# Raising the rank of all splits out of PSUM and of the heads' sums, in a two-layer transformer block on one core

## The chip, the cores and the metric

The kernel runs on one core of a Trainium2 chip. The metric is the time of one execution in device microseconds. Five engines work side by side, each through a queue of its own in order: TensorE (PE, the matrix engine, with its weight loads PEld), VectorE (DVE), ScalarE (ACT), GpSimd (POOL) and SyncE (SP), which here only issues DMA transfers. Matrix products are accumulated in PSUM; everything else lies in SBUF.

## The reference

Two layers of a hybrid block over a latent stream x of 512 tokens (8 rows of a grid of 64 columns) and a context stream of 256 tokens, 1024 features each. Cut to what matters:

```python
h  = modulate(rms_norm(x, norm_pre1), sh1, sc1)        # adaln sums from c @ w_ada
q, k, v, u, cq, ckv, kr, g = split_cols(h @ w_in, IN_SIZES)
o_na   = na_latent(q, k, v, k_ctx, v_ctx, rpb)         # 8 heads of 64: window 8x16, and the context
o_pool = pool_mixer(u, pool_w, pool_scale)
o_mla  = mla_attend(q_nope, q_rope, k_nope_all, k_rope_all, v_all)   # 8 heads, 768 keys
y = merge_branches(o_na, o_pool, o_mla, g) @ w_o       # sigmoid gates
x = x + g1 * rms_norm(y, norm_post1)
h2 = modulate(rms_norm(x, norm_pre2), sh2, sc2)
x = x + g2 * rms_norm(conv_ffn(h2), norm_post2)        # up to 2*2816, conv of 3, gelu, down
```

The context stream goes through the same in the first layer; in the second only its keys and values are used.

## The kernel before

Products need nearly float32 accuracy, so each operand is split in two float32r tiles: hi, a rounding of the value, and lo, what is left. A product is three matmuls (hi by lo, hi by hi, lo by hi). A split is a pair: ScalarE casts hi, then VectorE subtracts hi from the value to give lo. `evac` does this for a value that lies in PSUM (in the last merge, for one in SBUF). `split` does it for weights and other values in SBUF, with the subtraction on VectorE or GpSimd by an estimate of their queues.

The order is made in two steps. While the program is written out, the class `Sched` keeps a rough clock and interleaves generators: streams of attention units, a dense stream (`dense`, a projection is 24 matrix steps over 512 and 256 tokens), and a background stream that sums up the next adaln vectors on VectorE (`adacc`, `adahi`, `adalo`). The order in which TensorE's instructions are written is the order that it keeps (`manual_schedule` for PE). For all other engines and the DMA queue a planner, when the kernel is built, plays the program through with its own estimates: at each moment it gives an engine the instruction of lowest rank among those that it believes ready. The rank is the place in the text. `tc.high_priority(HP)` with HP = 100 ranks what it encloses 100 places earlier. The queues that result are fixed; on the chip each engine waits for the first instruction in its own.

Stages of a layer, in order, with the names of the profile:

- pooling branch (ups, pwps) with gates (gps) and its merge (mps);
- windowed attention, 8 heads: q, k, v (qps, kps, vps), v transposed (vtps, split to vt). A unit has scores S, softmax in P (maxima mx, sums sx, their reciprocal rs; Pc for context units), four transposes of P (tps), a split to PT, and products ops (opc) which hold both halves of a head's output in 64 partitions each. `gather` adds them: ScalarE copies one half to osum, VectorE adds the other. Three streams of units run at a time. S, tps, ops, opc and vtps share four PSUM buffers ("p1"); projections have two of their own ("mm");
- gates and merge of that branch (tgn, acn); latent projections (cps);
- second attention (MLA), 8 heads over 768 keys: projections in pieces pps, split to qh and ql, kh and kl; V. A score unit has S in the two "mm" buffers, a maximum mxm on VectorE, an exponential P<-S on ScalarE, and a scaling P<-P on ScalarE, VectorE or GpSimd. `apply` transposes P (tps), splits it to pth and ptl, and makes po, whose halves are added in om (copy o on ScalarE, sum on VectorE). tps, pps, rps and po share four buffers;
- merge (mps, acm, split to mhi and mlo), output projection yps with its square sq and scaled y, and a chain for each 128 tokens: xt, square, rstd on GpSimd, ht, eight transposes hps, split to mhi and mlo. The first FFN products f2ps begin as soon as 256 tokens are there;
- FFN (ffps, cv, gh and gl, dps), and the same token chain at its end.

In the kernel before, raised ranks stand in the scores (`na_unit`, `na_ctx_unit`, `scores`) and at sq and y of the output projection. The splits of `evac` and the sums in `gather` and `apply` have the plain rank.

Of the kernel before, what the change touches and what calls it, by code (L numbers as in the profile page):

```python
# [8 lines left out]
F32 = mybir.dt.float32  # L9
F32R = mybir.dt.float32r  # L10
AF = mybir.ActivationFunctionType
ALU = mybir.AluOpType
# [13 lines left out]
HP = 100  # L26
# [215 lines left out]
def body(tc, I, out):  # L242
    sch = Sched()
    nc = _NC(sch, tc.nc)
    es = ExitStack()

    def mm(out, lhsT, rhs, start, stop):
        n = 1
        for d in rhs.shape[1:]:
            n *= d  # L250
        sch.pe(max(n, 256) * 0.4167 + 2.5 if rhs.dtype == F32R else max(n, 16) * 1.667, out.name, [lhsT.name, rhs.name])
        nc.tensor.matmul(out=out, lhsT=lhsT, rhs=rhs, start=start, stop=stop)  # L252

    def tr(out, in_):
        sch.pe(109, out.name, [in_.name])
        nc.tensor.transpose(out=out, in_=in_, identity=ident)  # L256
# [126 lines left out]
                yield 0  # L383

    def evac(ps, hi, lo, scale=None):
        if scale is None:
            nc.scalar.copy(out=hi, in_=ps)
            nc.vector.tensor_sub(out=lo, in0=ps, in1=hi.bitcast(F32))
        else:
            nc.scalar.activation(out=hi, in_=ps, func=AF.Copy if isinstance(scale, float) else AF.Identity, scale=scale)  # L390
            nc.vector.scalar_tensor_tensor(out=lo, in0=ps, scalar=scale, in1=hi.bitcast(F32),
                                           op0=ALU.mult, op1=ALU.subtract)

    def rstd_of(ss, ss2=None):
        r = sm.tile([128, 1], F32, tag="rstd", name="rstd")
# [70 lines left out]
    def norm_to_h(xt, A, B, pool, hhi, hlo, tt):  # L466
        ss = sm.tile([128, 1], F32, tag="ss", name="ss")
        t = pool.tile([128, D], F32, tag="ht", bufs=2, name="ht")
        nc.scalar.activation(out=t, in_=xt, func=AF.Square, accum_out=ss)
        r = rstd_of(ss)  # L470
        nc.vector.scalar_tensor_tensor(out=t, in0=xt, scalar=r, in1=A, op0=ALU.mult, op1=ALU.mult)
        nc.vector.tensor_add(out=t[:, :BC], in0=t[:, :BC], in1=B[:, :BC])
        nc.gpsimd.tensor_add(out=t[:, BC:], in0=t[:, BC:], in1=B[:, BC:])
        for g in range(2):
            yield Need([t], [P1])
            ps = ps1.tile([128, 512], F32, tag="p1", name="hps")
            for k in range(4):
                tr(ps[:, k * 128:(k + 1) * 128], t[:, (4 * g + k) * 128:(4 * g + k + 1) * 128])
            pv = ps.rearrange("p (k c) -> p k c", k=4)
            evac(pv, hhi[:, 4 * g:4 * g + 4, tt * 128:(tt + 1) * 128], hlo[:, 4 * g:4 * g + 4, tt * 128:(tt + 1) * 128])  # L480
# [6 lines left out]
    def transpose_n(P, n):  # L487
        ps = ps1.tile([128, 512], F32, tag="p1", name="tps")
        for i in range(n):
            tr(ps[:, i * 128:(i + 1) * 128], P[:, i * 128:(i + 1) * 128])  # L490
        return ps
# [158 lines left out]
    for l in range(NL):  # L650
# [79 lines left out]
        def pool_mix(g):  # L730
            def run(_):
                ps = pmm.tile([128, 1024], F32, tag="mm", name="pwps")
                yield from mm3(ps, *pool_d[g], 1, TQ)
                evac(ps[:, :TQ], ophi[:, g], oplo[:, g], pscale[:, g:g + 1])
            return run
# [43 lines left out]
        def na_vt(p):  # L779
            def run(_):  # L780
                v = qkvt[p, "v"]
                vt = na.tile([128, 10, 2, 2, 64], F32R, tag="vt", bufs=2, name="vt")
                srcs = [v[:, 8 * BAND0[j] + 128 * hf:8 * BAND0[j] + 128 * hf + 128] for j in range(4) for hf in range(2)]
                srcs += [v[:, SX + i * 128:SX + (i + 1) * 128] for i in range(2)]
                for i0 in range(0, 10, 4):
                    tp = ps1.tile([128, 512], F32, tag="p1", name="vtps")
                    n = min(4, 10 - i0)
                    for i in range(n):
                        tr(tp[:, i * 128:(i + 1) * 128], srcs[i0 + i])
                    tv = tp[:, :n * 128].rearrange("p (k e c) -> p k e c", k=n, e=2)  # L790
                    evac(tv, vt[:, i0:i0 + n, :, 0, :], vt[:, i0:i0 + n, :, 1, :])
                qkvt[p, "vt"] = vt
                yield 0
            return run
# [17 lines left out]
        def gather(po, e, hi, lo, shape):  # L812

            t = na.tile([128, 512], F32, tag="osum", bufs=1, name="osum")
            rows = slice(64 * e, 64 * e + 64)
            nc.scalar.copy(out=t[0:64], in_=po[64:128])
            nc.vector.tensor_add(out=t[0:64], in0=po[0:64], in1=t[0:64])
            v = t[0:64].rearrange("p (u h c) -> p u h c", u=2, h=2)
            o = na.tile([128, 2, 128], F32, tag="ohead", bufs=1, name="ohead")
            nc.gpsimd.tensor_add(out=o[rows], in0=v[:, :, 0, :], in1=v[:, :, 1, :])  # L820
            ov = shape(o[rows])
            nc.scalar.copy(out=hi[rows], in_=ov)
            nc.vector.tensor_sub(out=lo[rows], in0=ov, in1=hi[rows].bitcast(F32))

        def na_unit(p, e, j):
# [35 lines left out]
            if left[u] == 0:  # L861
                c = slice(4 * (j // 2), 4 * (j // 2) + 4)
                gather(ops, e, rowm(nahi[:, p, :SX])[:, c], rowm(nalo[:, p, :SX])[:, c],
                       lambda x: x.rearrange("p u (b r c) -> p (u b) r c", b=2, r=8))
# [225 lines left out]
        om = mp.tile([128, 4, TQ], F32, tag="om", name="om")  # L1090
# [146 lines left out]
        def apply(hd, qp):  # L1237
            e = hd % 2
            wide = qp < 2
            us = [(hd, qp, 0), (hd, qp, 1)] if wide else [(hd, qp, None)]  # L1240
            yield lambda: all(u in ptile for u in us)
            Ps = [ptile[u] for u in us]
            pth, ptl = [ml.tile([128, 6, 256], F32R, tag=t, bufs=2, name=t) for t in ("pth", "ptl")]
            nkt = 6 if wide else 2
            if wide:
                for q2 in range(2):
                    yield Need([Ps[q2]], [P1])
                    tp = transpose_n(Ps[q2], 4)
                    tv = tp.rearrange("p (k c) -> p k c", k=4)
                    evac(tv, pth[:, 0:4, q2 * 128:(q2 + 1) * 128], ptl[:, 0:4, q2 * 128:(q2 + 1) * 128])  # L1250
            yield Need(Ps, [P1])
            tp = ps1.tile([128, 512], F32, tag="p1", name="tps")
            for i in range(2):
                for q2 in range(2):
                    c0 = (4 + i) * 128 if wide else q2 * 256 + i * 128
                    tr(tp[:, (2 * i + q2) * 128:(2 * i + q2 + 1) * 128], Ps[q2 if wide else 0][:, c0:c0 + 128])
            evac(tp.rearrange("p (k c) -> p k c", k=2), pth[:, nkt - 2:nkt], ptl[:, nkt - 2:nkt])
            flow["t"] += len(us)
            yield Need([pth, ptl], [P1])
            rn = slice(64 * e, 64 * e + 64)  # L1260
            po = ps1.tile([128, 512], F32, tag="p1", name="po")
            n = 0
            k0 = 0 if wide else 4
            for i in range(nkt):
                for t in (pth, ptl):
                    mm(out=po[:, 0:256], lhsT=V[:, k0 + i, hd, :], rhs=t[:, i, :], start=n == 0, stop=n == 2 * nkt - 1)
                    n += 1
            o1 = ml.tile([128, 256], F32, tag="o1", bufs=1, name="o1")
            nc.scalar.copy(out=o1[0:64], in_=po[64:128, 0:256])
            nc.vector.tensor_add(out=om[rn, hd // 2, qp * 256:qp * 256 + 256], in0=po[0:64, 0:256], in1=o1[0:64])  # L1270
            yield 0

        def sstream():
# [7 lines left out]
        def tstream():  # L1281
            yield lambda: "v" in hready
            while pairs_:
                yield from apply(*pairs_.pop(0))
# [403 lines left out]
```

## Time and profile before

| | us |
|---|---|
| median of 3 runs | 2472.48 (2471.0 to 2478.62) |
| the profiled execution's own time | 2472.59 |
| its span, first to last instruction | 2470.8 |
| PE busy | 2380.2 |
| DVE busy | 1530.0 |
| ACT busy | 1029.2 |
| POOL busy | 643.3 |

The mean granted TensorE clock is 0.99. Busy times of engines overlap. A group of rows names tiles as out<-in; L252 is the line of the helper that issues matmuls, L256 that of transposes, L207 that of all instructions which go through the recording wrapper, so tiles tell them apart.

### The profile page before, as it was taken

How to read it: one execution, taken by the hardware profiler on the slowest of the kernel's cores; microseconds unless marked ns; L12 is line 12 of the kernel's file. 1: busy time of each engine (PE TensorE's matmuls, PEld its weight loads, DVE VectorE, ACT ScalarE, POOL GpSimd, SP SyncE). 2: the span in 40 equal slices, each digit the busy share in tenths (PEclk: the TensorE clock that was granted, in tenths of full speed). 3: DMA queues.
4: the chain of work that ended last, by engine and by line, in shares of the span. 5: the costliest groups of instructions: out<-in, count | busy, mean ns of one | idle time of the engine just before them, and what ended most of it. 6: DMA issues, size and time to landing. Idle time of an engine off the chain costs nothing. (4 is left out here: it accounts for less than half of the span.)

```text
span 2470.8 us, 33534 instructions
## 1 busy us (share of the span) xinstructions
PE 2380.2 (96%) x12868; PEld 2016.2 (82%) x12868; DVE 1530.0 (62%) x2458; ACT 1029.2 (42%) x1820; POOL 643.3 (26%) x470
## 2 busy tenths in 40 slices
PE   8999999999989999999999999999999999999998
PEld 6888888888878788888888878888887888888886
DVE  7746877774678566866653466276644786444444
ACT  5313655421566343332223243265523763533332
POOL 4312232352112233222231153022242132122212
PEclk9999999999999999999999999999999999999999
DMA  6343233325423443444422142323234344422222
GB/s 248 116 137 114 95 103 111 109 91 166 111 74 108 164 152 107 155 145 137 128 69 69 51 172 95 127 76 93 81 107 140 88 135 170 130 94 94 94 85 94
DMA packets 98744, 286.31 MB, mean 116 GB/s; under 512 B 12340, under 2 KB 13748, under 8 KB 98584
## 3 DMA queue, kind: packets, MB, share of 16 engines
q1 hardware_dynamic: 98584, 284.17, 35.3%
q8 instruction: 102, 1.67, 0.3%
q14 instruction: 58, 0.48, 0.1%
HBM read 244.73 MB, written 25.23 MB: 109 GB/s over the span
## 5 line engine op out<-in xcount | busy, mean ns | idle before, releaser
L207 ACT CAST whi<-raw 128x1024 fp32r<-128x1024 f32 (+1 forms) x212 | 218.8, 1033 | 442.4 <-PE gps L252 153.2
L207 POOL TENSOR_TENSOR wlo<-raw,whi 128x1024 fp32r<-128x1024 f32 (+2 forms) x90 | 215.4, 2394 | 593.0 <-ACT whi L207 554.3
L207 DVE TENSOR_TENSOR wlo<-raw,whi 128x1024 fp32r<-128x1024 f32 (+1 forms) x122 | 158.1, 1296 | 236.3 <-ACT whi L207 235.7
L252 PE MATMUL ffps<-mlo,whi 128*128 128x512 f32 x992 | 300.0, 358 | 2.5 <-DVE cv L207 2.5
L252 PE MATMUL ffps<-mhi,whi 128*128 128x512 f32 x992 | 299.8, 357 | 0.0
L252 PE MATMUL ffps<-mhi,wlo 128*128 128x512 f32 x992 | 299.8, 357 | 0.0
L207 DVE SCALAR_TENSOR_TENSOR cv<-ffps,cw,cv 128x511 f32<-128x511 f32 x248 | 159.0, 655 | 140.4 <-ACT cv L207 137.0
L207 DVE SCALAR_TENSOR_TENSOR adacc<-rawa,st,adacc 128x512 f32<-128x512 f32 x224 | 194.6, 889 | 23.7 <-DMA rawa<-in_w_ada 20.9
L252 PEld LDWEIGHTS ffps<-mlo,whi 128*128 128x128 f32 x992 | 164.6, 189 | 34.2 <-issue 2.1
L252 PEld LDWEIGHTS ffps<-mhi,whi 128*128 128x128 f32 x992 | 163.6, 189 | 29.4
L252 PEld LDWEIGHTS ffps<-mhi,wlo 128*128 128x128 f32 x992 | 163.6, 189 | 29.4
L252 PE MATMUL dps<-wdl,gh 128*128 128x512 f32 x440 | 174.7, 397 | 2.3 <-ACT dps L207 1.9
L252 PE MATMUL dps<-wdh,gl 128*128 128x512 f32 x440 | 174.5, 396 | 0.9 <-POOL gl L207 0.9
L252 PE MATMUL dps<-wdh,gh 128*128 128x512 f32 x440 | 174.0, 395 | 0.0
L207 POOL TENSOR_TENSOR gl<-cv,gh 128x768 fp32r<-128x768 f32 (+1 forms) x44 | 70.1, 1594 | 368.0 <-ACT gh L207 330.1
L207 DVE TENSOR_TENSOR y<-dps,y 128x1024 f32<-128x1024 f32 (+1 forms) x70 | 74.5, 1068 | 67.7 <-PE dps L252 67.7
L256 PE MATMUL tps<-ident,P 128*128 128x128 f32 x672 | 95.7, 275 | 15.4 <-DVE ptl L207 5.3
L207 ACT CAST wdh<-wdr 128x512 fp32r<-128x512 f32 x88 | 53.6, 620 | 129.6 <-PE dps L252 98.6
L252 PE MATMUL gps<-hlo,whi 128*128 128x512 f32 (+1 forms) x384 | 100.2, 342 | 3.8 <-ACT tg L207 1.6
L252 PEld LDWEIGHTS dps<-wdl,gh 128*128 128x128 f32 x440 | 82.8, 188 | 24.5 <-ACT dps L207 3.7
L256 PEld LDWEIGHTS tps<-ident,P 128*128 128x128 f32 x672 | 76.6, 140 | 30.3 <-issue 6.5
L252 PEld LDWEIGHTS dps<-wdh,gl 128*128 128x128 f32 x440 | 82.7, 188 | 21.3 <-POOL gl L207 1.3
(360 smaller groups left out, 5770.9 us busy)
## 6 DMA issues: line engine op xcount, KB each, us to landing
raw<-in_w_in SPq DMA_DIRECT2D x94, 512.0 KB
raw<-in_w_up SPq DMA_DIRECT2D x88, 512.0 KB
rawa<-in_w_ada SPq DMA_DIRECT2D x80, 512.0 KB
wdr<-in_w_down SPq DMA_DIRECT2D x88, 256.0 KB
raw<-in_w_br SPq DMA_DIRECT2D x24, 512.0 KB
raw<-in_w_ada SPq DMA_DIRECT2D x16, 512.0 KB
wor<-in_w_o SPq DMA_DIRECT2D x32, 256.0 KB
modt<-moda SPq DMA_DIRECT2D x16, 512.0 KB
```

The lines of the kernel that those rows point to most:

```text
L207: r = f(*a, **kw)
L252: nc.tensor.matmul(out=out, lhsT=lhsT, rhs=rhs, start=start, stop=stop)
L256: nc.tensor.transpose(out=out, in_=in_, identity=ident)
```

## The change

The two instructions of `evac`, the two of the sum in `gather`, and the two of the sum in `apply` are put into `tc.high_priority(HP)`, as the scores are already. Instructions, engines, tiles and TensorE's order are the same.

```diff
     def evac(ps, hi, lo, scale=None):
-        if scale is None:
-            nc.scalar.copy(out=hi, in_=ps)
-            nc.vector.tensor_sub(out=lo, in0=ps, in1=hi.bitcast(F32))
-        else:
...
+        with tc.high_priority(HP):
+            if scale is None:
+                nc.scalar.copy(out=hi, in_=ps)
+                nc.vector.tensor_sub(out=lo, in0=ps, in1=hi.bitcast(F32))
+            else:
...
@@ gather
-            nc.scalar.copy(out=t[0:64], in_=po[64:128])
-            nc.vector.tensor_add(out=t[0:64], in0=po[0:64], in1=t[0:64])
+            with tc.high_priority(HP):
+                nc.scalar.copy(out=t[0:64], in_=po[64:128])
+                nc.vector.tensor_add(out=t[0:64], in0=po[0:64], in1=t[0:64])
@@ apply
-            nc.scalar.copy(out=o1[0:64], in_=po[64:128, 0:256])
-            nc.vector.tensor_add(out=om[rn, hd // 2, qp * 256:qp * 256 + 256], in0=po[0:64, 0:256], in1=o1[0:64])
+            with tc.high_priority(HP):
+                nc.scalar.copy(out=o1[0:64], in_=po[64:128, 0:256])
+                nc.vector.tensor_add(out=om[rn, hd // 2, qp * 256:qp * 256 + 256], in0=po[0:64, 0:256], in1=o1[0:64])
```

## Rows read from the trace of the kernel before

**Rows 1.** The page, part 1: busy us (share of the span), instructions.
```profile
PE 2380.2 (96%) x12868; PEld 2016.2 (82%) x12868; DVE 1530.0 (62%) x2458; ACT 1029.2 (42%) x1820; POOL 643.3 (26%) x470
```

**Rows 2.** Windows, layer 0's attentions: length, busy by engine, PEclk, DMA share, GB/s.
```profile
196.00:510.00 314.00, 297.46 (x1831) 262.94 (x1829) 227.05 (x506) 159.13 (x358) 89.79 (x67) 0.99 0.32 107
...
620.00:800.00 180.00, 165.46 (x1026) 143.83 (x1025) 131.73 (x237) 117.81 (x241) 35.65 (x23) 0.97 0.36 98
```

**Rows 3.** Waits of PE, whole kernel: total us, times, longest.
```profile
PE S L252 <- DVE mx L207: 6.9, 6, 2.0
PE tps L256 <- DVE ptl L207: 5.3, 7, 1.0
...
PE f2ps L252 <- DVE mlo L207: 4.2, 2, 3.3
...
PE S L252 <- ACT P L207: 3.8, 6, 1.6
...
PE tps L256 <- ACT Pc L207: 2.7, 1, 2.7
...
PE tps L256 <- DVE rs L207: 2.3, 1, 2.3
PE ops L252 <- DVE mx L207: 2.2, 1, 2.2
...
PE tps L256 <- DVE om L207: 2.0, 1, 2.0
...
PE ops L252 <- DVE PT L207: 2.0, 4, 0.5
PE pps L252 <- DVE om L207: 1.9, 1, 1.9
...
PE hps L256 <- DVE mlo L207: 1.9, 3, 0.9
```

**Rows 4.** Timeline about 665 us, ACT, DVE, POOL, PE: start, us, instruction.
```profile
666.65 0.91 ACT L207 ACTIVATE P<-S,mxm 128x768 f32<-128x768 f32 x1
...
667.54 0.93 ACT L207 ACTIVATE P<-P,mxm 128x768 f32<-128x768 f32 x1
668.49 0.37 ACT L207 COPY o<-po 64x256 f32<-64x256 f32 x1
...
664.70 0.62 DVE L207 TENSOR_SCALAR P<-P,mxm 128x768 f32<-128x768 f32 x1
...
667.88 1.20 DVE L207 TENSOR_SCALAR P<-P,mxm 128x768 f32<-128x768 f32 x1
...
669.60 0.40 DVE L207 TENSOR_TENSOR om<-po,o 64x256 f32<-64x256 f32 x1
...
666.83 1.83 POOL L207 TENSOR_TENSOR wlo<-raw,whi 128x768 fp32r<-128x768 f32 x1 [20.81 <-ACT whi L207]
...
665.81 0.28 PE L252 MATMUL po<-ptl,V 128*128 128x256 f32 x1
```

**Rows 5.** Windows behind two waits; granted clock after the POOL column.
```profile
670.00:673.00 3.00, 2.94 (x12) 2.71 (x13) 2.58 (x7) 1.69 (x6) 0.00 (x0) 0.58 1.01 205
673.00:676.00 3.00, 3.00 (x19) 2.73 (x18) 0.66 (x2) 1.23 (x3) 0.00 (x0) 0.85 0.84 243
...
2084.20:2087.00 2.80, 2.77 (x13) 2.77 (x14) 2.80 (x4) 0.00 (x0) 1.85 (x3) 0.50 0.00 0
2087.00:2091.00 4.00, 4.00 (x23) 4.00 (x23) 1.87 (x2) 1.53 (x3) 0.74 (x2) 0.57 0.35 135
```

**Rows 6.** Timeline before layer 1's FFN, ACT and DVE.
```profile
2081.25 1.05 ACT L207 CAST mhi<-hps 128x512 fp32r<-128x512 f32 x2
...
2082.29 1.28 DVE L207 SCALAR_TENSOR_TENSOR ht<-xt,rstd,modt 128x1024 f32<-128x1024 f32 x1 [2.13 <-ACT mhi L207]
2083.49 0.68 DVE L207 TENSOR_TENSOR mlo<-hps,mhi 128x512 fp32r<-128x512 f32 x1
```

**Rows 7.** Timeline at 1955 us, DVE (two maxima merged).
```profile
1955.19 1.81 DVE L207 TENSOR_REDUCE mxm<-S 128x1 f32<-128x768 f32 x2
```

More of the change, by code (lines that the diff above doesn't have):

```diff
@@ L385, in evac @@
     def evac(ps, hi, lo, scale=None):
-        if scale is None:
-            nc.scalar.copy(out=hi, in_=ps)
-            nc.vector.tensor_sub(out=lo, in0=ps, in1=hi.bitcast(F32))
-        else:
-            nc.scalar.activation(out=hi, in_=ps, func=AF.Copy if isinstance(scale, float) else AF.Identity, scale=scale)
-            nc.vector.scalar_tensor_tensor(out=lo, in0=ps, scalar=scale, in1=hi.bitcast(F32),
-                                           op0=ALU.mult, op1=ALU.subtract)
+        with tc.high_priority(HP):
[3 more added lines that the diff above has]
+            else:
+                nc.scalar.activation(out=hi, in_=ps, func=AF.Copy if isinstance(scale, float) else AF.Identity, scale=scale)
+                nc.vector.scalar_tensor_tensor(out=lo, in0=ps, scalar=scale, in1=hi.bitcast(F32),
+                                               op0=ALU.mult, op1=ALU.subtract)
     def rstd_of(ss, ss2=None):
```

## The prediction

> **What bounds the kernel now.** I read the page's first part before anything else: the matrix engine is busy for 2380.2 of 2470.8 us [rows 1]. The change adds and removes no instruction, so it can win only from that engine's idle time and from the slow clock that follows it. Then comes the table by stage, for where the splits and sums work: the first layer's windowed attention has 16.5 us of idling (314.00 less 297.46), its second attention 14.5 us (180.00 less 165.46), with VectorE busy for some 73% of either [rows 2]. Last come the matrix engine's waits over the whole kernel: the reader is to see which of the names are splits out of PSUM (PT, ptl, mlo), which are sums (om), and which belong to the scores (mx, Pc, rs, and P from ScalarE) [rows 3].
>
> In the second attention the waits on a split or sum are the longer ones: tps on ptl 5.3 us, tps on om 2.0, pps on om 1.9, against 3.8 us of S on the scores' exponential [rows 3]. Four PSUM buffers carry the transposes, products and projections there, and each comes free only when VectorE has read it. A late split or sum therefore holds the matrix engine, which goes through its instructions in a fixed order.
>
> **What the change does.** The planner fills each queue from what it believes ready at one time, lowest rank first; a raised block ranks 100 places earlier in the text. Only the scores had this. Now the splits and sums have it too: towards the scores they stand in the order of the text again, and they pass what is not raised (weight splits, the scaling of P by its sum, copies, the adaln sums). TensorE's order is written out and stays. No DMA is added or moved; SyncE only sees a weight buffer come free later by what its split is held up.
>
> *Two long waits on a sum.* From 665 to 670 us the queue can be followed. The last matmul of po starts at 665.81. ScalarE then runs an exponential from 666.65 and the scaling of P from 667.54 (0.93), and only at 668.49 the copy of po (0.37); VectorE's sum om follows at 669.60 and ends at 670.00 [rows 4], and pps has waited 1.9 us for it [rows 3]. Raised, the copy passes the scaling. If it still stands behind the exponential it starts at about 667.6, and om at about 668.0 in place of 669.6: 1.6 us. The other such wait, 2.0 us of tps on om [rows 3], I count at half, 1.0 us, since VectorE may have begun a scaling when the copy ends. These stalls also cost clock: behind the first the granted clock is 0.58 over 3 us and 0.85 over the next 3 [rows 5], a mixture of the levels of 1.2 and 2.4 GHz, so 0.42 x 3 + 0.15 x 3 = 1.7 us of full-speed time. I take that once whole and once half, 2.6 us. Together 5.2 us; bounds 0 (the planner saw the copy ready too late to choose it) and 1.9 + 2.0 + 2 x 1.7 = 7.3 us.
>
> *The token chain before layer 1's FFN.* f2ps waits 3.3 us for mlo in one piece [rows 3]. ScalarE casts mhi from 2081.25 (two casts, 1.05 together), but VectorE takes the next token's ht first (1.28 from 2082.29) and splits mlo at 2083.49 [rows 6]. Raised, mlo can start when the first cast ends, about 2081.8: 1.7 us less. If the casts, too, pass what stands ahead of them, all 3.3 us go. What is late then is ht, by up to two splits of 0.68 us; f2ps gives the matrix engine work meanwhile. Behind the wait the clock is 0.50 over 2.8 us and 0.57 over 4 us [rows 5], which is 1.4 + 1.7 = 3.1 us. I take 1.7 and half of the clock, 3.2 us; bounds 0 and 6.4 us.
>
> *The short waits.* The rest of rows 3 that ends on a split: S on mx 6.9, tps on ptl 5.3, ops on mx 2.2, ops on PT 2.0, hps on mlo 1.9, and 0.9 of f2ps on mlo (4.2 less 3.3), 19.2 us. Where the windowed attention names mx, the split PT stands just before it on VectorE, so I count these here. What a raise returns differs from wait to wait. At 1955 us two maxima (1.81 us) stand in front of the ptl for which tps then waits 1.0 us [rows 3, 7], and that would go whole; elsewhere the split already starts when its cast ends, and nothing goes. I take a third, 6.4 us; bounds 0 and 19.2 us.
>
> *What is late instead.* A split ahead of a maximum holds an exponential up by 0.68 us, and with it the buffer of S. I let the 3.8 us of S on P grow by as much again, and add a third of the 5.0 us in which tps waits for softmax pieces (Pc 2.7, rs 2.3) [rows 3]: 5.5 us. Bounds are 0 and, at 0.68 us for each of the second attention's 72 score units (40 and 32), 49 us; I stay near the bottom, as only 6 waits of S on P exist. Weight splits cost nothing while a projection's 24 matrix steps lie between one and its use; without that cover each costs the length of what passes it, a cast of 0.5 us. Behind whi on ScalarE waits POOL's wlo, and behind that on POOL ohead and adalo; they slip by the same 0.5 us.
>
> One row speaks against displacing work. The scaling of P that takes 0.62 us at 664.70 takes 1.20 at 667.88, beside a POOL split that runs from 666.83 to 668.66 [rows 4]; this costs 0.58 us wherever a scaling is moved beside POOL. The Trainium skill (SBUF — State Buffer, section "SBUF: two separate sides") puts it as an exclusive lock: GpSimd and a VectorE operation in a two-port mode, or with two SBUF inputs, hold each other off for the whole instruction. The trace agrees with it so far as the scaling ends just after POOL does. By the row ten displaced scalings take 6 us from the sum; by the rule each could wait a whole POOL split, and ten would take three times that. The sum below has none of it, and it is a rival.
>
> **Sum.** 5.2 + 3.2 + 6.4 - 5.5 = 9.3 us gained, taken from the profiled execution's 2472.6 us (span 2470.8 and 1.8 around it; the runs' median of 2472.5 is the same): 2463.3 us.
>
> **Rivals.** *Handed on:* the waits end earlier, but the next link (a maximum, an exponential, an ht) comes later by as much, or the order hardly moves since the planner sees only one of the two ready when it chooses. For it: VectorE's total work stays, at 131.73 of 180.00 us [rows 2]. Against it: in rows 4 the copy of po is ready for two of ScalarE's instructions. Time 2466 to 2479, middle 2471.
>
> *Scores behind splits,* the other side. In the second attention S has two buffers, freed by an exponential that itself waits for a 0.9 us maximum. If many units pay 0.68 us for a ptl in front, that outgrows the 14.8 us of the three gains. It decides at (14.8 + 7.4) / 0.68 = 33 of the 72 units; with 45 paying, 2472.6 - 14.8 + 30.6 = 2488 us. For it: the scores alone were ahead so far. Against it: few waits of S on P.
>
> *Scalings beside POOL:* POOL is busy for 89.79 of 314.00 and 35.65 of 180.00 us in layer 0's attention [rows 2]. If ten scalings that ran free now fall there and each is waited for, the time is 2463.3 + 5.8 = 2469 us. By the Trainium skill's rule (SBUF — State Buffer, as above), at a POOL split of 1.83 us each, it would be 2482 us.
>
> **How the numbers follow.** Forecast 0.55; handed on 0.26; scores behind splits 0.13; scalings beside POOL 0.06. A measurement of this kernel can't tell less than about 0.3%, 7.4 us, from no change, so faster 0.55, same 0.32, slower 0.13. The forecast's own range is 2444 to 2465: at its low end both long terms reach their bounds (13.7 us), most of the short waits go (15 us), and displacement costs nothing. Further down nothing is left to win but idle time of other causes. For 8 in 10 the upper end takes in what is handed on, to 2479; above it lies the scores' case, and below 2444 a few in a hundred.
>
> **What would show it.** Right: no wait of 1 us or more on om; a clock of 1.00 where rows 5 have 0.58; f2ps waiting under 2 us on mlo; ScalarE's o copies ahead of the scalings of P; idle time in the two stages of rows 2 down from 31 to some 24 us. Wrong: waits of S on P of more than 10 us, tps waiting for a scaling, or new stalls of 2 us with a clock near 0.6 behind them: one such costs about 3.7 us, and three undo the forecast.

## The result and the profile after

The changed kernel takes 2486.13 us (median of 9 runs, 2480.14 to 2489.98) against 2473.34 us for the kernel before (9 runs on the same chip). The ratio is 1.0055, 95% interval 1.0041 to 1.0069: slower by 0.55%, about 13.6 us. The forecast was 2463.3 us, faster.

The page's first line, as [rows 1], shows the same work to within 5 us on every engine, in a span of 2484.3 us:

```profile
PE 2381.4 (96%) x12868; PEld 2016.7 (81%) x12868; DVE 1531.0 (62%) x2458; ACT 1028.3 (41%) x1820; POOL 638.5 (26%) x470
```

TensorE's instructions are the same in the same order in all kernels here, so a stretch can be bounded by the same two matmuls in each. By such windows (columns as in [rows 2]), the first two rows answer to [rows 2], the next two are layer 1's windowed and second attention:

```profile
198.52:508.71 310.19, 297.21 (x1832) 261.94 (x1830) 226.21 (x506) 158.16 (x358) 90.27 (x67) 0.99 0.33 108
618.49:800.39 181.90, 163.77 (x1026) 144.32 (x1024) 131.24 (x238) 118.00 (x241) 35.44 (x23) 0.97 0.35 95
1578.93:1818.16 239.23, 228.86 (x1303) 194.96 (x1302) 140.84 (x347) 128.02 (x285) 54.35 (x43) 1.00 0.27 89
1908.13:2083.60 175.47, 164.37 (x941) 140.95 (x940) 132.52 (x209) 112.62 (x214) 39.32 (x25) 0.99 0.44 134
```

and layer 1's two in the kernel before:

```profile
1577.00:1810.00 233.00, 227.27 (x1304) 195.19 (x1303) 140.02 (x347) 128.84 (x285) 53.57 (x43) 1.00 0.29 91
1900.00:2068.00 168.00, 163.88 (x941) 139.25 (x940) 129.57 (x209) 112.85 (x214) 39.18 (x25) 1.00 0.46 140
```

Only layer 0's windowed attention became shorter, by 4 us; the second attention is 1.9 us longer (the idle time of the two together stays at 31 us, 13.0 and 18.1, where 24 was forecast), and layer 1's two are, between the same matmuls, 6.3 and 7.6 us longer, most of it idle time of the matrix engine (5.7 to 10.4 us and 4.1 to 11.1 us, length less PE busy). The prediction's table of stages has layer 0 alone [rows 2]. The rest is 2.8 us more in the token stretch between the two layers, 1.4 and 1.8 us less around the token chains before the two FFNs, and 2.5 us more at the very start. There the queues of all kernels here are the same but for a few instructions, and the profiled executions take 191.6 to 200.9 us, so these 2.5 us say nothing.

The matrix engine's waits over the whole kernel, as [rows 3]:

```profile
PE S L252 <- ACT P L207: 9.6, 10, 3.4
PE hps L256 <- DVE ht L207: 6.9, 8, 1.9
PE tps L256 <- POOL P L207: 6.5, 3, 2.9
PE tps L256 <- DVE P L207: 5.1, 5, 2.6
PE S L252 <- DVE PT L207: 4.7, 6, 1.2
...
PE f2ps L252 <- DVE mlo L207: 3.7, 2, 2.7
...
PE ops L252 <- DVE PT L207: 2.6, 6, 1.3
...
PE tps L256 <- DVE sx L207: 2.2, 3, 1.4
PE tps L256 <- ACT P L207: 2.1, 2, 1.9
...
PE vtps L256 <- ACT P L207: 1.9, 2, 1.6
...
PE gps L252 <- DVE kl L207: 1.6, 3, 0.6
...
PE po L252 <- DVE ptl L207: 1.5, 2, 0.9
...
PE pps L252 <- DVE om L207: 1.3, 1, 1.3
...
PE tps L256 <- DVE ptl L207: 1.1, 2, 0.9
```

What was to go went: tps no longer waits for om, pps waits 1.3 us for it, tps on ptl fell from 5.3 to 1.1. What stands first now is the softmax: P from ScalarE, VectorE and POOL, under four names, holds the matrix engine for 23.3 us (9.6 + 6.5 + 5.1 + 2.1), where the kernel before had 3.8, nothing, 0.3 and 0.2.

Four places show how. At 665 us the timeline, as [rows 4], went as predicted, and better:

```profile
665.77 0.91 ACT L207 ACTIVATE P<-S,mxm 128x768 f32<-128x768 f32 x1
...
666.79 0.37 ACT L207 COPY o<-po 64x256 f32<-64x256 f32 x1
667.00 1.19 DVE L207 TENSOR_SCALAR P<-P,mxm 128x768 f32<-128x768 f32 x1
...
668.11 0.41 DVE L207 TENSOR_TENSOR om<-po,o 64x256 f32<-64x256 f32 x1
...
668.62 0.96 ACT L207 ACTIVATE P<-P,mxm 128x768 f32<-128x768 f32 x1
```

The copy of po comes right behind the exponential, ScalarE's scaling only after it, and pps is released at 668.57 where it was 670.

At 729 us the timeline shows six splits in one row ahead of two maxima:

```profile
728.57 3.66 DVE L207 TENSOR_TENSOR ptl<-tps,pth 128x512 fp32r<-128x512 f32 x6
...
732.15 1.53 DVE L207 TENSOR_REDUCE mxm<-S 128x2 f32<-128x512 f32 x2
...
733.77 0.90 ACT L207 ACTIVATE P<-S,mxm 128x768 f32<-128x768 f32 x1
...
733.93 1.95 PE L252 MATMUL S<-K,Q 128*128 128x512 f32 x6 [3.38 <-ACT P L207]
```

Before, three splits stood ahead of these maxima,

```profile
734.80 1.87 DVE L207 TENSOR_TENSOR ptl<-tps,pth 128x512 fp32r<-128x512 f32 x3
```

and the wait was 1.6 us, the longest in its group of [rows 3]: 1.8 us more of splits, 1.8 us more of wait. At 768 us it is the other end of the softmax that is late:

```profile
763.01 0.21 ACT L207 ACTIVATION_READ_ACCUMULATOR P<-S,mxm 128x1 f32 x1
...
768.79 0.27 DVE L207 RECIPROCAL mxm<-mxm 128x1 f32<-128x1 f32 x3
...
769.13 4.77 POOL L207 TENSOR_SCALAR P<-P,mxm 128x768 f32<-128x768 f32 x2 [9.09 <-PE po L252]
...
771.78 0.60 PE L256 MATMUL tps<-ident,P 128*128 128x128 f32 x2 [2.65 <-POOL P L207]
```

Three reciprocals that were due at different times run together, once VectorE has nothing raised left; ScalarE had read out the sum of the first one's exponential by 763.22, 5.6 us earlier (the first row). In the kernel before, the same unit's reciprocal runs 0.04 us after that readout (it ends at 766.62), and POOL's scaling starts right behind it, at 766.99:

```profile
766.66 0.16 DVE L207 RECIPROCAL mxm<-mxm 128x1 f32<-128x1 f32 x1 [0.53 <-ACT P L207]
```

Taken in order over all 72 score units, the reciprocal comes more than 1 us after its readout 11 times, by up to 5.6 us; in the kernel before it does so 3 times, by up to 2.6. The other two waits on POOL's P, at 2016.94 and 2022.89, also follow such reciprocals, which are 5.2 and 4.7 us late.

Behind such stalls the granted clock is what the prediction feared (the column after POOL's): 0.52 behind the one at 771.78, and 0.57 behind one of 2.6 us at 781.72 and behind the one at 733.93. The last is not new: behind the wait of 1.6 us in the kernel before, the clock is 0.57 as well (738.40 to 741.00). Behind the wait on om that was shortened, the first row, it is 1.00 where [rows 5] have 0.58 and 0.85:

```profile
670.46:673.09 2.63, 2.63 (x19) 2.32 (x18) 1.45 (x5) 2.05 (x7) 0.00 (x0) 1.00 0.98 196
771.80:775.00 3.20, 3.20 (x16) 3.20 (x17) 1.37 (x2) 1.62 (x3) 2.10 (x1) 0.52 0.00 0
733.93:737.00 3.07, 3.07 (x13) 2.83 (x14) 1.88 (x5) 1.85 (x4) 0.00 (x0) 0.57 0.20 46
2099.15:2102.00 2.85, 2.85 (x15) 2.85 (x16) 2.76 (x4) 0.00 (x0) 1.68 (x3) 0.60 0.00 0
```

The last row is the chain before layer 1's FFN, which hardly changed. As in [rows 6], ht still stands ahead of mlo:

```profile
2097.21 1.28 DVE L207 SCALAR_TENSOR_TENSOR ht<-xt,rstd,modt 128x1024 f32<-128x1024 f32 x1 [2.13 <-ACT mhi L207]
2098.41 0.68 DVE L207 TENSOR_TENSOR mlo<-hps,mhi 128x512 fp32r<-128x512 f32 x1
...
2099.15 0.39 PE L252 MATMUL f2ps<-mlo,whi 128*128 128x256 f32 x1 [2.75 <-DVE mlo L207]
```

### The profile page after: what moved, and what is told of

Its sections match the earlier page's. It is cut to its first block, busy times and chain, and to the rows that moved or that the text cites. A ratio compares the mean times of both kernels' runs of the same rounds, so it can differ in the third digit from the quotient of the medians.

```text
span 2484.3 us, 33528 instructions
## 1 busy us (share of the span) xinstructions
PE 2381.4 (96%) x12868; PEld 2016.7 (81%) x12868; DVE 1531.0 (62%) x2458; ACT 1028.3 (41%) x1820; POOL 638.5 (26%) x470
```

## The experiments

All start from the changed kernel. For taking a raise back, `evac` got an argument: `hp=0` is the old rank. Each was timed in 6 to 12 runs against runs of the kernel before on the same chip, whose medians were 2472.05 to 2473.18 us. "Stages" are the lengths in us, in one profiled execution, of the two windowed attentions (layers 0 and 1) and the two second attentions (0 and 1).

| Kernel | median us | ratio to before (95%) | windowed 0, 1 | second 0, 1 |
|---|---|---|---|---|
| before | 2473.3 | | 314.2, 232.9 | 180.0, 167.9 |
| the change | 2486.1 | 1.0055 (1.0041 to 1.0069) | 310.2, 239.2 | 181.9, 175.5 |
| 1 softmax tail raised too | 2483.2 | 1.0047 (1.0035 to 1.0060) | 310.6, 240.2 | 179.8, 173.3 |
| 2 second attention at old rank | 2475.9 | 1.0014 (1.0004 to 1.0025) | 310.5, 240.1 | 177.1, 168.1 |
| 3 raise in second attention only | 2483.1 | 1.0043 (1.0028 to 1.0058) | 315.8, 233.0 | 181.8, 177.5 |
| 4 maxima, exponentials at 200 | 2481.9 | 1.0035 (1.0021 to 1.0049) | 311.5, 239.3 | 179.5, 172.0 |
| 5 chain at 200 | 2482.8 | 1.0040 (1.0025 to 1.0055) | 313.6, 240.1 | 178.6, 172.8 |
| 6 sums only | 2466.4 | 0.9973 (0.9960 to 0.9986) | 313.0, 232.5 | 173.8, 167.9 |
| 7 Q and K splits too | 2488.3 | 1.0060 (1.0047 to 1.0074) | 312.9, 236.8 | 182.0, 179.5 |
| 8 turned P only (second att.) | 2479.8 | 1.0033 (1.0021 to 1.0046) | 314.5, 233.0 | 179.5, 173.9 |
| 9 pieces only | 2472.0 | 0.9998 (0.9983 to 1.0013) | 318.0, 233.0 | 176.5, 167.6 |
| 10 sums and tail | 2471.0 | 0.9987 (0.9973 to 1.0001) | 312.7, 232.6 | 175.2, 170.4 |
| 11 windowed splits only | 2476.2 | 1.0015 (1.0002 to 1.0028) | 317.3, 235.4 | 177.0, 168.2 |
| 12 token splits only | 2474.9 | 1.0009 (0.9995 to 1.0022) | 315.4, 232.9 | 177.0, 168.7 |
| 13 chain at 200, narrow maximum too | 2478.8 | 1.0039 (1.0022 to 1.0056) | 310.4, 239.2 | 177.0, 171.1 |
| 14 sums, narrow maximum | 2467.7 | 0.9977 (0.9964 to 0.9990) | 316.4, 232.6 | 174.1, 167.7 |
| 15 change, narrow maximum | 2482.2 | 1.0047 (1.0033 to 1.0061) | 310.3, 239.2 | 175.6, 177.4 |

The stages have a spread of their own, to be kept in mind below. It shows where kernels have the same queues on every engine, but for one instruction at most. With before's queues layer 0's second attention takes 180.0, 177.1, 177.0 and 177.0 us (before, 2, 11, 12) and layer 1's 167.9, 168.1, 168.2 and 168.7. With the change's queues layer 0's takes 181.9, 181.8 and 182.0 us (the change, 3, 7) and layer 1's 175.5, 177.5, 179.5 and 177.4 (the change, 3, 7, 15). So 3 to 4 us in one such stage may be chance, and by the means of these groups the second attentions lose some 13 us where the one pair of profiles shows 9.5. Layer 1's windowed attention repeats within 1 us. What decides is the ratio, and a named wait that comes or goes.

**1. The tail of the softmax.** The reciprocal and the scaling of P, which had no raise, get it.

```diff
+            with tc.high_priority(HP):
                 nc.vector.reciprocal(out=mx[:, 4:4 + nz], in_=mx[:, 2:2 + nz])
                 for z, (a, b) in enumerate(parts_):
                     ...
```

> The changed kernel, and in the second attention the reciprocal of a score's sum and the scaling of P by it get the raised rank too. Theory A (the raised splits pass the unraised end of the softmax, and TensorE's transposes wait for P; about 12 of the 13.6 us lost come from that): the waits of tps on a scaling of P (6.5 us on POOL's, 5.1 on VectorE's, 2.1 on ScalarE's) fall below 4 us in all, and the time falls to about 2474 us (2468 to 2480). Rival B (the scores' maximum and exponential stand behind splits): the 9.6 us of S on P stay or grow, and the time stays at 2483 to 2490 us. Rival C (the planner's estimates are off anywhere it reorders): some other time, no pattern.

The three waits of tps on POOL's P shrink to one of 0.2 us and those on VectorE's from 5.1 to 2.9 us, but S on P grows from 9.6 to 13.0 us and po now waits 2.5 us for an om. The two second attentions are 4.3 us shorter, the ratio 1.0047. So the late tail is real, and not the bulk: the waits fell as theory A had it, the time is that of rival B, and my first theory was too large.

**2 and 3. Where.** The raise is taken back in the second attention, or kept there alone.

```diff
-                        evac(r[0], hi[:, a:b], lo[:, a:b])
+                        evac(r[0], hi[:, a:b], lo[:, a:b], hp=0)
   ... (V, pth/ptl twice, and the sum om likewise)
```

> The changed kernel with the raise taken back in the second attention (splits of pieces, V and transposed P, and the sum om): what is left is the windowed attention, the token chains, the pooling branch and the merge. Theory A: the second attention costs about 8 us of the 13.6 (2.3 in layer 0, 5.7 in layer 1), so 2478 us (2474 to 2482), with the second layer's windowed attention still 6 us longer than before. Rival B says the same place, by another cause. Rival C: the loss does not sit in a stage, 2480 to 2488 us.

> The raise in the second attention alone; the splits and sums elsewhere have the plain rank. Theory A: waits of tps on scalings of P as in the changed kernel, time 2473 + 8 = 2481 us (2477 to 2486). Rival C: within 3 us of before.

Both times lie in the ranges of theory A, and the two add up: +0.14% and +0.43% against +0.55% (3.5 + 10.6 = 14.1 us for 13.6). Three quarters of the loss are the second attention's.

**4 and 5. Put the chain ahead again.** In 4 the second attention's maxima and exponentials are raised by 200, in 5 the reciprocal and scaling too.

```diff
-                with tc.high_priority(HP):
+                with tc.high_priority(2 * HP):
                     nc.vector.tensor_reduce(out=mx[:, 0:1], ...)
```

> The changed kernel with the second attention's maxima and exponentials raised by 200 places in place of 100, so that they are ahead of the splits as they were before. Rival B: S on P falls back from 9.6 us to about 4 and the time to 2475 us (2470 to 2480). Theory A: the scalings of P are still unraised and now have two kinds of work ahead of them, so tps still waits for them and the time is 2482 to 2492 us.

> The changed kernel with the second attention's whole softmax chain (maximum, exponential, reciprocal, scaling of P) ranked 200 ahead, so that it stands before the splits again, as the maximum and exponential did before the change, and the reciprocal and scaling too. Theory C (the loss in the second attention is only that the splits pass the softmax chain, all of its links): what the second attention loses (7.8 us in the second part of layer 0's, 7.6 us in layer 1's) is gone, the gain of 6 us from the sums and splits in layer 0's first part stays, and what the windowed attention and the pooling branch of layer 1 lose (6.3 and 2.8 us) stays: 2471 to 2475 us, waits of S on P under 5 us. Rival D (VectorE's work is full there, whoever stands first makes another late): the waits move to ptl in front of po and tps, at least 6 us of them, and the time is 2479 to 2484.

Both take some 6 us from the two second attentions. Kernel 4, at 2481.9 us, lies at the low edge of what theory A gave. Kernel 5 does not reach what theory C gave: it is rival D's case, in time and in waits. Waits on ptl of tps and po come back, 3.0 and 1.0 us, and so does a wait of tps on mxm, 3.0 us in four, that is of the same kind. Each of the four ends behind a ptl that stands behind two maxima; a reciprocal of 0.15 us right behind the ptl gives it its name. The longest, 0.95 us until 1970.50, has on VectorE

```profile
1967.94 1.81 DVE L207 TENSOR_REDUCE mxm<-S 128x1 f32<-128x768 f32 x2
...
1969.67 0.68 DVE L207 TENSOR_TENSOR ptl<-tps,pth 128x512 fp32r<-128x512 f32 x1
```

That makes 7 us of waits on a late turned P, where rival D had at least 6. S on P is still 7.4 us, with the wait of 3.4 us unmoved.

**6. The sums alone.** All splits go back, `osum` and `om` stay raised.

```diff
-    evac(tp..., pt[:, :, 0, :], pt[:, :, 1, :])
+    evac(tp..., pt[:, :, 0, :], pt[:, :, 1, :], hp=0)
   ... (every evac likewise)
```

> The changed kernel with every split back at its old rank: only the sums osum and om are raised. Theory: the waits of tps and pps on om (2.0 and 1.9 us) and the slow clock behind them go without a cost, as a sum is one copy and one addition per head and pair: about 4 us faster than before, 2468 us, with no wait on S for P above the 3.8 us of before. Rival: a sum displaces a scaling or a maximum like a split does, and the time is that of before, 2471 to 2474.

Faster than before, 0.9973 (0.9960 to 0.9986): 6.7 us. Its waits:

```profile
PE tps L256 <- DVE ptl L207: 6.8, 10, 1.1
...
PE S L252 <- DVE osum L207: 4.3, 6, 1.2
...
PE S L252 <- ACT P L207: 2.5, 4, 1.6
```

S on P is below the 3.8 us of before, tps on om is gone, as its theory had it; the price is 1.5 us more of tps on ptl, 2.1 of po on ptl, and 2.3 of Sc on vt. In the windowed attention the longest waits on mx, 2.2 of ops and 2.0 of S, became 1.4 and 1.2 on osum, and the 2.3 us of tps on rs went.

**7. Q and K too.** The split of Q and K in the windowed attention, which is written out and not an `evac`, is raised as well.

```diff
+                            with tc.high_priority(HP):
                                 hi = place(z[e])
                                 nc.scalar.copy(out=hi[a], in_=src[a])
                                 ...
```

> The changed kernel with the split of Q and K in the windowed attention raised as well (the one split out of PSUM that the change left at its old rank). Theory: in layer 1's windowed attention, which lost 6.3 us, the waits of gps on kl (1.6 us in three) and the slow clock behind them go, so that stage loses 3 to 4 us less and the time is 2482 to 2483. Rival: the loss there comes from the exponentials that now run later (vtps on P 1.6, tps on sx 1.4, tps on P 1.1), and putting still more ahead of them makes it no better: 2486 to 2490.

The waits of gps on kl go and layer 1's windowed attention takes 236.8 us in place of 239.2, as the theory had it; the time does not fall and is the rival's (the second attention's 4 us more are of the spread above). The 2.4 us are not those of kl alone, as a wait of 1.1 us of tps on a scaling of P goes with them (it is taken up under the rivals below). No gain is shown.

**8, 9, 11, 12. One kind of split each, no sums.** Turned P in the second attention; the projected pieces K, Q and V there; V and turned P in the windowed attention; tokens and pooling outputs. The edits are `hp=0` on all others.

> Only the splits of the transposed P in the second attention are raised; every other split and all sums are back at the old rank. Theory (these splits are what passes the softmax chain): the second part of layer 0's second attention loses some 6 us and layer 1's second attention some 6 us, the waits on om stay at 3.9 us, and the time is 2480 to 2485. Rival (the splits of the projected pieces, 512 and 256 columns of K, Q and V, do it): the two stages stay within 2 us of before, and the time is 2471 to 2475.

> Only the splits of the projected pieces of the second attention (K, Q and V; 512 or 256 columns each) are raised; the turned P, every other split and all sums are at the old rank. The sums alone gained 6.6 us in the second attentions, the turned P alone lost 5.6, all three together lost 9.1. Theory (a split of any name costs there, and the costs add): this loses some 10 us in the two second attentions and takes 2478 to 2484 us. Rival (the pieces are few, and the rest came from splits and sums meeting): within 3 us of before, 2470 to 2475.

> Only the splits of V and of the turned P in the two windowed attentions are raised; every other split and all sums are at the old rank. Theory (splits delay the exponentials there as well, the sum osum gave the gain): layer 1's windowed attention loses the 6 us that it lost in the changed kernel, and layer 0's keeps under 2 us of its 4: 2474 to 2478. Rival (the loss in layer 1 comes from osum going ahead of the splits): layer 1's stage within 2 us of before, 2468 to 2473.

> Only the splits outside the attentions are raised (the turned tokens into hhi and hlo, the mixed pooling outputs, the halved tokens mhi and mlo). Theory (the token ht that hps turns next is passed by the splits, and the wait moves from mlo to ht): the 2.8 us that the stretch before layer 1's windowed attention lost in the changed kernel are there, the wait of f2ps on mlo falls by 0.5 us only, and the time is 2473 to 2476. Rival (the wait on ht comes from elsewhere): 2470 to 2472.

The turned P costs 8.2 us (0.33%): S on P is 8.2 us, the time, 2479.8, lies just under the theory's range, and layer 1's second attention is 6.0 us longer as expected, while layer 0's is not. The waits on om, which were to stay, are gone with no sum raised, and pps waits 3.2 us for ptl where it waited 1.0. The pieces cost nothing; my theory of costs that add up for any split was wrong there. The windowed splits cost 3.7 us (0.5 to 6.9), and in layer 1 2.5 us of the 6.3. The token splits show 3.1 us in the token stretch between the layers (its waits are named under the rivals below), while the time is not told from before. Summed with the sums' gain, 8.2 - 0.5 + 3.7 + 2.2 - 6.7 = 6.9 us of the 13.6; with some 3 us of uncertainty on each, it is not shown whether the rest is more than chance, but layer 1's windowed attention (2.5 and -0.4 apart, 6.3 together) says that sums and splits raised together cost more.

**10. Sums and the softmax tail.**

```diff
   (kernel 6, and)
+            with tc.high_priority(HP):
                 nc.vector.reciprocal(...)
```

> The kernel with only the sums raised (2466.4 us), and the reciprocal and scaling of P in the second attention raised too. Theory (the tail of the softmax was late in the changed kernel only because splits stood before it): here no split passes it, so raising it gains nothing: 2465 to 2469, the same as the sums alone. Rival (the tail is late in any order, and tps waits for it): 2 to 5 us less, 2461 to 2464.

0.9987: no gain over the sums alone; if anything a loss of 3.5 us, the size of the uncertainty. The rival is refuted. The median is 2 us above the theory's range too, and S on P is 6.9 us where kernel 6 has 2.5.

**13 to 15. The link that nobody had raised.** The six splits at 729 us stand ahead of a maximum with two columns: that of the 256-column units, which exists in layer 0 only, eight times, and stands outside the raised block in every kernel so far, before included.

```diff
+                with tc.high_priority(HP):        # 2 * HP in 13
                     nc.vector.tensor_reduce(out=mx[:, 0:2], in_=S[:, 0:512]..., negate=True)
```

> As the kernel with the softmax chain 200 ahead (2482.8 us), and the one link of that chain that had no raised rank in any kernel so far, the maximum of the 256-column units (two queries' tiles in one, eight units, layer 0 only), put 200 ahead too. Theory (the splits pass this maximum, and S waits 3.4 us for the exponential behind it where it waited 1.6 before): that wait is 1.6 us or less, layer 0's second attention is 2 to 4 us shorter, and the time is 2478 to 2481. Rival (it is one place of many): 2481 to 2484.

> The kernel with only the sums raised (2466.4 us), and the maximum of the 256-column units raised by 100 as the other maxima are. Theory: the wait of S on P of 1.6 us at the unit of the fourth head goes, with some of the slow clock behind it: 2463 to 2465. Rival (the maximum takes the place of a split for which tps then waits): 2466 to 2469.

> The changed kernel (2486.1 us) with the maximum of the 256-column units raised by 100 as well, so that the splits no longer pass it. Theory: the 3.4 us wait of S on P falls by 1.8 us or more, some of the slow clock behind it goes, and the time is 2482 to 2484. Rival: the splits still stand ahead of the wide maxima and the scaling, and what is won is lost at the next wait: 2485 to 2488.

In kernel 13 the same place reads

```profile
729.59 0.68 DVE L207 TENSOR_REDUCE mxm<-S 128x2 f32<-128x512 f32 x1
...
731.46 0.67 DVE L207 TENSOR_TENSOR ptl<-tps,pth 128x512 fp32r<-128x512 f32 x1
...
734.13 2.08 PE L252 MATMUL S<-K,Q 128*128 128x512 f32 x6
```

with no wait in front of S, and over the whole kernel

```profile
PE tps L256 <- DVE mxm L207: 4.8, 7, 1.0
PE tps L256 <- DVE ptl L207: 4.6, 7, 1.0
...
PE S L252 <- ACT P L207: 3.0, 6, 1.0
```

S on P is back below the 3.8 us of before, and the two second attentions take 348.1 us together, as before's 347.9, where the change takes 357.4 (kernels 2, 11 and 12, with before's queues, take 345.1 to 345.7). Here too all seven waits on mxm end behind a ptl: tps waits 9.4 us for a late ptl, where it waits 5.9 in the kernel before by the same count and 1.1 in the change. Its ratio of 1.0039 cannot be told from kernel 5's 1.0040; the median is 4 us lower. In kernel 15 the one maximum makes the stage that it stands in 6.3 us shorter (181.9 to 175.6, with 181.8 and 182.0 in kernels 3 and 7), and the median falls by 4 us, as its theory had it; the intervals overlap. In kernel 14 the wait goes, tps waits 0.9 us for ptl and 0.7 us for om in its place, and the time is that of kernel 6: the rival there.

## Why the prediction was wrong, by its own steps

*The two waits on a sum* (5.2 us). Right. The one went whole (2.0 us), the other fell from 1.9 to 1.3, and the clock behind it was 1.00 in place of 0.58 and 0.85, worth the 1.7 us worked out there: 4.3 us. So the sign "no wait of 1 us or more on om" was missed by the 1.3 us. Kernel 6 shows that this gain stands by itself.

*The token chain* (3.2 us). Wrong: f2ps waits 2.7 us instead of 3.3. The step "Raised, mlo can start when the first cast ends" failed; ht kept its place ahead of mlo on VectorE, which idles until 2097.21 although the first of the two casts from 2096.17 (1.05 us together) is over by about 2096.7; why the planner left it so is not shown. Kernels 9 and 11, in which these splits are at their old rank, gain 1.2 and 1.5 us between the same matmuls around it where the change gains 1.8.

*The short waits* (6.4 us). The gain was larger: tps on ptl lost 4.2 us, S on mx of 6.9 became S on PT of 4.7, ops on mx and PT together fell from 4.2 to 2.6, and hps no longer waits for mlo (1.9): some 10 us. One reading of the rows was wrong: PT stands right before mx in five of these seven waits; before the longest, 2.2 us of ops on mx, stands adab, and before one of 0.6 us osum.

*What is late instead* (5.5 us) is the step that failed. By the same list the new or longer waits are S on P 5.8 us more, tps on P of POOL, VectorE and ScalarE 13.2 more (6.5 + 4.8 + 1.9), hps on ht 3.8, tps on sx 2.2, gps on kl 1.6, po on ptl 1.2, vtps on P 0.8: 28.6 us. Gains of some 15 us (4.3 + 0.6 + 10) less 28.6 make a loss of 14, and 13.6 were measured. These are picked rows, but the whole list agrees: it has 80.2 us of waits before and 93.0 in the change, 12.8 more, and PE busy, in which the slow clock lies, is 1.2 us more [rows 1]. The step was wrong in three ways. It stayed "near the bottom, as only 6 waits of S on P exist": but these waits were few because the maxima and exponentials stood ahead, and the change takes just that away. Kernel 13 gives it back, and the waits are as few again (though ptl is then late, as above). It priced a split ahead of a maximum only; the reciprocal and the scaling at the end of the chain had no raise and were passed by splits, sums and maxima alike, and the turned P can't start without them (kernel 1: these waits go when they are raised). And it took layer 1's attentions, with more than all of the loss, from layer 0's rows.

*Rivals.* "Scores behind splits" came nearest in size, 2488 us for 2486.1, and the turned P alone (kernel 8) shows its mechanism at 8.2 us. Its own signal, S on P above 10 us, was just missed at 9.6, since the scaling carried the larger part; its other two signs, tps waiting for a scaling and stalls of over 2 us with a clock near 0.6 behind them, both came. "Handed on" holds for mlo and ht: where two splits pass ht in the token stretch, the timeline of the change has, on VectorE and POOL,

```profile
1465.09 1.27 DVE L207 TENSOR_TENSOR mlo<-hps,mhi 128x512 fp32r<-128x512 f32 x2
1466.28 1.28 DVE L207 SCALAR_TENSOR_TENSOR ht<-xt,rstd,modt 128x1024 f32<-128x1024 f32 x1
...
1468.09 1.54 DVE L207 TENSOR_TENSOR ht<-ht,modt 128x704 f32<-128x704 f32 x1
...
1467.95 0.93 POOL L207 TENSOR_TENSOR ht<-ht,modt 128x320 f32<-128x320 f32 x1
```

and hps then waits 1.9 us, the longest of its group. Before, ht's second part took 0.89 us, with POOL's part behind it. This is "Scalings beside POOL" in another place: VectorE's 704 columns end 0.75 us after POOL's 320, so they ran, for the most part, behind them. The Trainium skill (SBUF — State Buffer, section "SBUF: two separate sides") has the port pair that the two engines share as locked for a whole instruction by whoever starts first; the trace agrees, as the 0.65 us added here fit, to 0.14 us, a wait until POOL ends at 1468.88. For the second attention's scalings of P the rival was not borne out: VectorE's 44 take 24.7 us where they took 25.2. In layer 1's windowed attention it was: two scalings by rs, of 0.49 us at the median, take 2.69 and 2.60 us beside a POOL split (in the kernel before the longest of this stage takes 0.79),

```profile
1679.99 2.69 DVE L207 TENSOR_SCALAR P<-P,rs 128x512 f32<-128x512 f32 x1
...
1680.02 2.38 POOL L207 TENSOR_TENSOR wlo<-raw,whi 128x1024 fp32r<-128x1024 f32 x1 [1.59 <-ACT whi L207]
```

and tps waits 1.1 us until the first is done. Its wait of 1.4 us on sx ends behind the second, which runs from 1775.06 to 1777.66 beside POOL's from 1775.00; only a one-column sx of 0.14 us stands between.

*What stays open.* Why layer 1's windowed attention loses 6.3 us with sums and splits together and 2.5 and nothing apart. The places are known (vtps on P 1.6 us, sx 1.4, P 1.1, kl 0.6, 0.6 and 0.4). Two of them, 2.5 us, are the scalings beside POOL just shown; in kernels 6 and 11 the longest scaling there takes 1.4 and 1.2 us. Kernel 7 removed the waits on kl and one of these two; no kernel took the others apart, so this is argued from the rows. And kernel 13, whose second attentions are about as long as before's, is still 0.39% slower: layer 1's windowed attention and the token stretch keep their 6.3 and 2.9 us, which makes most of that.

## What to carry to other kernels

A wait list made under a priority shows the slack that the priority made, not the slack that is there: when others are raised to the same rank, price the old holder as if it had none, over its whole chain up to the instruction that the matrix engine needs. Raise what is rare and ends a chain first: here one copy and one addition per head and pair gave 6.7 us, while the splits cost some 20 on top. When a chain is raised, look for the links outside the block; here the reciprocal, the scaling and the maximum of the eight narrow units were. Raising those as well won back little (kernels 1, 5 and 13 are still 0.39 to 0.47% slower than before): the chain put ahead makes the splits late that share VectorE with it.

## What the runs showed of the hardware

POOL's scaling of P, 2.20 to 2.39 us in the kernel before, takes 3.00 us at 2013.89 in the changed one, where VectorE runs omlo and a scaling from 2013.70 on, and VectorE's next omlo, from 2014.89, takes 1.24 us in place of 0.67. So far as these rows show, either engine can be the one that is held up. And identical queues on every engine gave 175.5 and 179.5 us for one stage, and 180.0 and 177.0 for another: with a kernel whose stalls are a microsecond long, stages of single executions can't be compared below that, though layer 1's windowed attention repeats within 1 us.
